# Pooled products of a hybrid decoder step: one fp32 product per chunk, or three float32r products of split operands

## The chip, the core and the metric

One core of a Trainium2 chip runs the whole kernel. The metric is the device time of one execution in microseconds (us). The engines are TensorE (PE, its weight loads PEld), VectorE (DVE), ScalarE (ACT), GpSimd (POOL) and SyncE (SP). SP, ACT and POOL issue the transfers, each in the order of its own queue.

## What is computed

One inference step of a decoder layer: 1024 prompt tokens and 8 sample tokens, model width 1024, all in fp32. An RMS norm and one projection feed two halves. One is sparse attention in three branches, with paged caches for the sample tokens. The other is a pooling mixer in four channel groups of 128, and it is what changes here:

```python
def pool_mixer(u_ext, n_out, w_pool, pool_scale):
    ...
    mean = (csum[:, le - n_out + 1:] - lo) / (end[:, None] - start).astype(f32)
    d = (mean - uf[:, le - n_out:]).reshape(n, n_out, N_POOL_GROUPS, POOL_GROUP_DIM)
    y = jnp.einsum('nlgc,gcd->nlgd', d, w_pool).reshape(n, n_out, D_POOL)
    return y * pool_scale

def combine(x, o_attn, za, o_pool, zp, w_out):
    a = o_attn * jax.nn.silu(za.astype(jnp.float32))
    b = o_pool * jax.nn.silu(zp.astype(jnp.float32))
    mix = jnp.concatenate([a, b], axis=-1).astype(x.dtype)
    return x + jnp.einsum('nlm,md->nld', mix, w_out)
```

The trailing windows of the four groups are 2, 4, 8 and 16 tokens; the sample tokens take their history from `state_pool`.

## The kernel before

**Exact products from rounded operands.** Nearly every product takes its operands as float32r. `split_w` (L142) makes a high part by a copy on ScalarE and a low part by a subtraction on VectorE, and three matmuls, high x high, high x low and low x high, add up in PSUM. The pooled product (L849) is the exception before the change: plain fp32 operands and one call of matmul per chunk.

**The stages.** Up to about 180 us the kernel normalizes and transposes the input, projects keys and values, compresses the cache and projects the queries. From about 180 to 285 us it runs the pooling groups (L801 to L859) and, between them, `decode` (L548), the attention of the sample tokens. From 285 us on come the prompt's attention units with the output projection as filler.

**A pooling group g.** `load_tile` (L387) loads and splits 128 columns of weights for u. `feat_unit` (L400) projects them in three token chunks of 384, 384 and 264 (CHUNKS), each 24 matmuls (L404 to L406) into one of two PSUM accumulators that `ps_any` (L71) takes in turns. ScalarE copies each into u (L808). Three transposes (L810 to L812) serve the new pool state; the third turns the state rows, spt, for the window sums of the sample tokens (us, L815 to L817). VectorE adds u to itself shifted, one to four times (L824), and makes dd, mean minus u (L832). Then zp is projected in the same three chunks (L842), and `silu2` (L409) forms the gate sz: a tanh on ScalarE (L411), a multiplication on VectorE (L412). The three pooled products (L849) follow, and bb is product x scale x gate: on VectorE for two chunks (L852), on ScalarE and GpSimd for the third (L856, L857). GpSimd stores bb to b_d in DRAM (L859). The output projection reads it back much later (`split_m`, L1022).

**Tiles.** Before, spt (L707) and pw (L709) are whole and are loaded once by SP; sz and bb hold all 1032 tokens, with one buffer each. The accumulators of the pooled products are three PSUM tiles, "tp".

**Decode.** For each pair of samples GpSimd fetches cache rows into kvx (an indirect gather, L640, or a plain transfer, L644), TensorE transposes the keys (L646), ScalarE copies the values (L651) and GpSimd subtracts (L652). kvx has four buffers.

**The order.** In these stages each engine's order is made by a planner: it simulates the program in time (`TCKW`, L15) and takes ready instructions by priority. Decode and the attention units have high priority (L716, L1176). At run time every engine works in the order so made. Pools are stacked, and a tile that lies where an older one lay waits for that one (`reuse_waits="tile"`).

Of the kernel before, what the change touches and what calls it, by code (L numbers as in the profile page):

```python
# [7 lines left out]
F32 = mybir.dt.float32  # L8
# [33 lines left out]
def hybrid_step_kernel(ctx, tc, xp, xs, ccmp, cslc, cwin, spool, ptab, norm_g, w_in, cmp_pe, cmp_w1,  # L42
# [17 lines left out]
    def ps_t(name="tp"):  # L60
        return psum.tile([128, 512], F32, name=name, tag="tp", bufs=3)
# [80 lines left out]
    def split_w(hi, lo, raw, eng=None):  # L142
        nc.scalar.activation(hi, raw, AF.Copy)
        (eng or nc.vector).tensor_sub(lo, raw, r32(hi))
# [255 lines left out]
    def feat_unit(hi, lo, c):  # L400
        t0, n = CHUNKS[c]
        p = ps_any()
        for k in range(8):
            nc.tensor.matmul(p[:, :n], hi[:, k, :], xh[c][:, k, :], start=k == 0, stop=False)  # L404
            nc.tensor.matmul(p[:, :n], hi[:, k, :], xl[c][:, k, :], start=False, stop=False)  # L405
            nc.tensor.matmul(p[:, :n], lo[:, k, :], xh[c][:, k, :], start=False, stop=k == 7)  # L406
        return p, t0, n
# [295 lines left out]
    pes = ExitStack()  # L703
    pu = pes.enter_context(tc.tile_pool(name="pu", bufs=1, side="right", reuse_waits="tile"))
    pp = pes.enter_context(tc.tile_pool(name="pp", bufs=1, side="right", reuse_waits="tile"))
    bb = pp.tile([128, TOK], F32, name="bb")
    spt = pp.tile([120, 512], F32, name="spt")  # L707
    nc.sync.dma_start(spt, spool.rearrange("b s c -> (b s) c"))
    pw = pp.tile([128, 4, 128], F32, name="pw")  # L709
    nc.sync.dma_start(pw, pool_w.rearrange("g c d -> c g d"))  # L710
    cnt = pp.tile([128, 16], F32, name="cnt")
    nc.gpsimd.iota(cnt, pattern=[[1, 16]], base=1, channel_multiplier=0, allow_small_or_imprecise_dtypes=True)
    nc.vector.reciprocal(cnt, cnt)
# [87 lines left out]
    for g in range(4):  # L801
        w = 2 << g
        hi, lo = load_tile(w_cols(C_U + g * 128))
        u = pu.tile([128, H0 + TOK], F32, name="u", bufs=2)
        nc.vector.memset(u[:, :H0], 0.0)
        for c in range(3):
            p, t0, n = feat_unit(hi, lo, c)
            nc.scalar.activation(u[:, H0 + t0:H0 + t0 + n], p[:, :n], AF.Copy)  # L808
        p = ps_t("ut")
        nc.tensor.transpose(p[:15, :128], u[:, H0 + T - 15:H0 + T], ident)  # L810
        nc.tensor.transpose(p[:NB, 128:256], u[:, H0 + T:H0 + TOK], ident)
        nc.tensor.transpose(p[:, 256:376], spt[:, g * 128:(g + 1) * 128], ident[:120, :120])  # L812
        nc.vector.tensor_copy(utok[:15, g * 128:(g + 1) * 128], p[:15, :128])
        nc.vector.tensor_copy(utoks[:, g * 128:(g + 1) * 128], p[:NB, 128:256])
        us = pp.tile([128, NB, 16], F32, name="us", bufs=2)  # L815
        nc.vector.tensor_copy(us[:, :, :15], p[:, 256:376].rearrange("p (b s) -> p b s", b=NB))
        nc.vector.tensor_copy(us[:, :, 15], u[:, H0 + T:H0 + TOK])  # L817
        cur = u
        step = 1
        k = 0  # L820
        while step < w:
            nx = pp.tile([128, H0 + TOK], F32, name=f"ws{k % 2}")
            nc.vector.memset(nx[:, :H0], 0.0)
            nc.vector.tensor_add(nx[:, H0:H0 + T], cur[:, H0:H0 + T], cur[:, H0 - step:H0 + T - step])  # L824
            cur = nx
            step *= 2
            k += 1
        nc.vector.tensor_reduce(cur[:, H0 + T:H0 + TOK], us[:, :, 16 - w:], axis=AX.X, op=OP.add)
        nc.vector.scalar_tensor_tensor(cur[:, H0:H0 + w - 1], cur[:, H0:H0 + w - 1], float(w),
                                       cnt[:, :w - 1], op0=OP.mult, op1=OP.mult)  # L830
        dd = cur[:, H0:]
        nc.vector.scalar_tensor_tensor(dd, dd, 1.0 / w, u[:, H0:], op0=OP.mult, op1=OP.subtract)  # L832
        if g == 2:
            load_q(0, 0)
            load_q(0, 1)
        if g == 3:
            for _ in stage1(*UNITS[0]):
                pass
        hi, lo = load_tile(w_cols(C_ZP + g * 128))
        sz = pu.tile([128, TOK], F32, name="sz")  # L840
        for c in range(3):
            p, t0, n = feat_unit(hi, lo, c)  # L842
            silu2(sz[:, t0:t0 + n], p[:, :n])
        if g:
            bb = pp.tile([128, TOK], F32, name="bb")
        for c in range(3):
            t0, n = CHUNKS[c]
            p = ps_t("yp")
            nc.tensor.matmul(p[:, :n], pw[:, g, :], dd[:, t0:t0 + n], start=True, stop=True)  # L849
            cs = slice(t0, t0 + n)  # L850
            if c < 2:
                nc.vector.scalar_tensor_tensor(bb[:, cs], p[:, :n], psc[:, g:g + 1], sz[:, cs],  # L852
                                               op0=OP.mult, op1=OP.mult)
            else:

                nc.scalar.activation(bb[:, cs], p[:, :n], AF.Copy, scale=psc[:, g:g + 1])  # L856
                nc.gpsimd.tensor_mul(bb[:, cs], bb[:, cs], sz[:, cs])  # L857
                nc.gpsimd.tensor_copy(bs_t[:, g, :], bb[:, T:])
        nc.gpsimd.dma_start(b_d[g], bb)  # L859
    tc.keep_in_program_order(nc.sync.dma_start(npool_p, utok[:15]))  # L860
    tc.keep_in_program_order(nc.sync.dma_start(npool_s[:, 14], utoks))
    pes.close()
# [419 lines left out]
```

## Time and profile before

| | |
|---|---|
| median of 3 runs | 639.88 us (638.89 to 640.13) |
| profiled execution | 638.69 us |
| its span | 637.0 us |
| TensorE busy in the span | 622.3 us, 98% |
| VectorE, ScalarE, GpSimd busy | 423.4, 367.3, 270.7 us |

The span runs from the first to the last instruction that the profiler shows; the 1.69 us between it and the execution's own time lie around it. Busy time counts an instruction from its start to its modelled end. On TensorE these overlap, so what a matmul costs in a stream is read from the distance between starts. In the waits, "who waited for whom" names the releaser that came last.

### The profile page before, as it was taken

To read this page: it belongs to the slowest core of one execution; us is meant where nothing else is said; L and a number is where in the kernel's file an instruction comes from. 1 tells how busy PE (TensorE), PEld (TensorE's weight loads), DVE (VectorE), ACT (ScalarE), POOL (GpSimd) and SP (SyncE) were. 2 spreads that over 40 slices of the span, in tenths; PEclk is the share of its full clock that TensorE was granted. 3 is DMA by queue.
4 is the path that set the end of the run, shared out by engine and by line. 5 is a ranking of instruction groups with operands and counts; after the bars stand their busy time and mean duration, and the time that the engine had idled before them with its cause. 6 is when DMAs were issued, how large, how long until landed. Compare 5 with 4: busy or idle time off the path is not lost.

```text
span 637.0 us, 12211 instructions
## 1 busy us (share of the span) xinstructions
PE 622.3 (98%) x4160; PEld 578.5 (91%) x4160; DVE 423.4 (66%) x1253; ACT 367.3 (58%) x947; POOL 270.7 (43%) x412
## 2 busy tenths in 40 slices
PE   8999999999999999999999999999999999999995
PEld 5999999999999899999899899789999988898895
DVE  6754234637364647466887999778978787877653
ACT  5654233526223333217887988777877777776652
POOL 6144004314035615005556767645554556444510
PEclk9999999999999999999999999999999999999999
DMA  8436106956224433333313357313113030101101
GB/s 281 152 90 157 34 1 201 314 196 181 74 79 133 138 102 95 92 110 101 100 35 99 100 182 214 107 30 101 37 50 100 18 100 16 67 19 67 51 2 66
DMA packets 63742, 65.13 MB, mean 102 GB/s; under 512 B 4488, under 2 KB 55120, under 8 KB 63640
## 3 DMA queue, kind: packets, MB, share of 16 engines
q1 hardware_dynamic: 53631, 44.55, 23.4%
q0 software_dynamic: 4000, 12.76, 6.2%
q10 hardware_dynamic: 6048, 7.05, 3.2%
q8 instruction: 33, 0.54, 0.4%
q14 instruction: 30, 0.24, 0.1%
HBM read 50.98 MB, written 15.68 MB: 105 GB/s over the span
## 4 chain that ended last, share of the span: by engine, by line
PE 93%; DVE 2%; ACT 1%; issue 1%; DMA 1%; POOL 1%; DVEq 0%; POOLq 0%; ACTq 0%
PE pj L1053 14%; PE S L777 10%; PE tp L902 9%; PE pa L404 7%; PE pa L406 7%; PE pa L405 7%; PE O L920 5%; PE O L919 5%; PE pa L277 4%; PE pa L275 3%; PE pa L276 3%; PE pj L979 2%; PE pj L980 2%; PE pj L981 2%; PE xtp_ps L230 1%; PE pj L1057 1%
## 5 line engine op out<-in xcount | busy, mean ns | idle before, releaser
L908 DVE TENSOR_TENSOR pl<-tp,ph 128x512 fp32r<-128x512 f32 (+1 forms) x136 | 89.9, 670 | 22.7 <-ACT ph L907 22.0
L777 PE MATMUL S<-KT,qt 128*128 128x320 f32 (+10 forms) x400 | 98.2, 346 | 3.0 <-DVE sm L736 3.0
L907 ACT ACTIVATE ph<-tp 128x512 fp32r<-128x512 f32 (+1 forms) x136 | 78.0, 580 | 38.3 <-PE tp L902 28.7
L404 PE MATMUL pa<-x,ws_hi 128*128 128x384 f32 (+1 forms) x288 | 93.7, 325 | 0.0
L406 PE MATMUL pa<-x,ws_lo 128*128 128x384 f32 (+1 forms) x288 | 92.9, 323 | 0.0
L405 PE MATMUL pa<-x,ws_hi 128*128 128x384 f32 (+1 forms) x288 | 92.7, 322 | 0.0
L1053 PE MATMUL pj<-wo,mh 128*128 128x512 f32 (+1 forms) x272 | 84.1, 387 | 0.0
L920 PE MATMUL O<-pl,V 128*128 128x256 f32 x264 | 75.7, 305 | 0.2
L919 PE MATMUL O<-ph,V 128*128 128x256 f32 x264 | 74.0, 296 | 0.0
L777 PEld LDWEIGHTS S<-KT,qt 128*128 128x128 f32 x400 | 63.7, 189 | 9.0 <-DVE sm L736 3.0
L796 POOL TENSOR_SCALAR Ps<-Ps,sm,gates 128x64 f32<-128x64 f32 (+5 forms) x88 | 62.9, 722 | 19.9 <-DVE sm L792 7.3
L789 ACT ACTIVATE Ps<-Ps,sm 128x64 f32<-128x64 f32 (+4 forms) x96 | 60.2, 628 | 16.4 <-DVE sm L736 14.8
L404 PEld LDWEIGHTS pa<-x,ws_hi 128*128 128x128 f32 x288 | 54.2, 188 | 0.5
L405 PEld LDWEIGHTS pa<-x,ws_hi 128*128 128x128 f32 x288 | 54.2, 188 | 0.4 <-issue 0.3
L406 PEld LDWEIGHTS pa<-x,ws_lo 128*128 128x128 f32 x288 | 54.2, 188 | 0.2
L277 PE MATMUL pa<-w_hi,x 128*128 128x256 f32 (+1 forms) x184 | 52.9, 288 | 1.2 <-DVE x L236 1.2
L275 PE MATMUL pa<-w_hi,x 128*128 128x256 f32 (+1 forms) x184 | 53.6, 292 | 0.0
L1053 PEld LDWEIGHTS pj<-wo,mh 128*128 128x128 f32 x272 | 47.2, 188 | 6.1 <-ACT mh L1205 0.3
L920 PEld LDWEIGHTS O<-pl,V 128*128 128x128 f32 x264 | 49.8, 189 | 3.1 <-DVE pl L908 0.6
L276 PE MATMUL pa<-w_lo,x 128*128 128x256 f32 (+1 forms) x184 | 52.4, 285 | 0.0
L1053 PE MATMUL pj<-wo,ml 128*128 128x512 f32 (+1 forms) x136 | 52.1, 383 | 0.0
L919 PEld LDWEIGHTS O<-ph,V 128*128 128x128 f32 x264 | 49.9, 189 | 1.8
(302 smaller groups left out, 1556.1 us busy)
## 6 DMA issues: line engine op xcount, KB each, us to landing
ws_raw<-in_w_in SPq DMA_DIRECT2D x32, 256.0 KB, 3.1
qt<-q_d SPq DMA_DIRECT2D x64, 128.0 KB, 2.9
x_t<-in_x_prompt SPq DMA_DIRECT2D x8, 512.0 KB
wo_raw<-in_w_out SPq DMA_DIRECT2D x8, 512.0 KB, 4.3
r<-in_x_prompt SPq DMA_DIRECT2D x8, 512.0 KB, 3.1
out<-r SPq DMA_DIRECT2D x7, 512.0 KB, 3.1
q_d<-qhl ACTq DMA_DIRECT2D x8, 384.0 KB, 4.0
out<-kvf ACTq DMA_DIRECT2D x5, 512.0 KB, 3.1
```

The source lines that it names most:

```text
L275: nc.tensor.matmul(p[:n, :cn], xh[c][:, k, ts_], hi[:, k, :cn], start=k == 0, stop=False)
L276: nc.tensor.matmul(p[:n, :cn], xh[c][:, k, ts_], lo[:, k, :cn], start=False, stop=False)
L277: nc.tensor.matmul(p[:n, :cn], xl[c][:, k, ts_], hi[:, k, :cn], start=False, stop=k == 7)
L404: nc.tensor.matmul(p[:, :n], hi[:, k, :], xh[c][:, k, :], start=k == 0, stop=False)
L405: nc.tensor.matmul(p[:, :n], hi[:, k, :], xl[c][:, k, :], start=False, stop=False)
L406: nc.tensor.matmul(p[:, :n], lo[:, k, :], xh[c][:, k, :], start=False, stop=k == 7)
L777: nc.tensor.matmul(S[:, :ln], qt[:, f, h, :], KT[:, kv, k0 + a:k0 + a + ln], start=f == 0, stop=f == 1)
L907: nc.scalar.activation(ph[:, :m], tp[:, :m], AF.Copy)
L908: nc.vector.tensor_sub(pl[:, :m], tp[:, :m], r32(ph[:, :m]))
L919: nc.tensor.matmul(O[:, :256], vv, ph[:, a * 256:(a + 1) * 256], start=False, stop=False)
L920: nc.tensor.matmul(O[:, :256], vv, pl[:, a * 256:(a + 1) * 256], start=False, stop=last)
L1053: nc.tensor.matmul(p, a[:, k % 4, :], w, start=first and kk == 0, stop=last and kk == 2)
```

## The change

The weights of the pooled product are loaded by group on GpSimd's queue (pwr) and split once per group (pw, now float32r with two parts). dd is split chunk by chunk into dx, and three float32r matmuls replace the fp32 one. The gate sz, the result bb and the store to b_d go by chunk, and chunk c's product now stands between zp's chunk c and chunk c + 1 in the program. The state rows spt are loaded by group, also by GpSimd. Buffers: spt 2, pwr 1, pw 1, sz 2, dx 1, bb 2.

```diff
-    bb = pp.tile([128, TOK], F32, name="bb")
-    spt = pp.tile([120, 512], F32, name="spt")
-    nc.sync.dma_start(spt, spool.rearrange("b s c -> (b s) c"))
-    pw = pp.tile([128, 4, 128], F32, name="pw")
-    nc.sync.dma_start(pw, pool_w.rearrange("g c d -> c g d"))
...
+        spt = pp.tile([120, 128], F32, name="spt", bufs=2)
+        nc.gpsimd.dma_start(spt, spool.rearrange("b s c -> (b s) c")[:, g * 128:(g + 1) * 128])
...
-        nc.tensor.transpose(p[:, 256:376], spt[:, g * 128:(g + 1) * 128], ident[:120, :120])
+        nc.tensor.transpose(p[:, 256:376], spt, ident[:120, :120])
...
+        pwr = pp.tile([128, 128], F32, name="pwr")
+        nc.gpsimd.dma_start(pwr, pool_w[g])
+        pw = pp.tile([128, 2, 128], F32R, name="pw")
+        split_w(pw[:, 0], pw[:, 1], pwr)
...
-        sz = pu.tile([128, TOK], F32, name="sz")
         for c in range(3):
+            sz = pu.tile([128, 384], F32, name="sz", bufs=2)
             p, t0, n = feat_unit(hi, lo, c)
-            silu2(sz[:, t0:t0 + n], p[:, :n])
-        if g:
-            bb = pp.tile([128, TOK], F32, name="bb")
-        for c in range(3):
-            t0, n = CHUNKS[c]
+            silu2(sz[:, :n], p[:, :n])
+            dx = pp.tile([128, 2, 384], F32R, name="dx")
+            split_w(dx[:, 0, :n], dx[:, 1, :n], dd[:, t0:t0 + n])
             p = ps_t("yp")
-            nc.tensor.matmul(p[:, :n], pw[:, g, :], dd[:, t0:t0 + n], start=True, stop=True)
-            cs = slice(t0, t0 + n)
+            for a, (f, d) in enumerate(((0, 0), (0, 1), (1, 0))):
+                nc.tensor.matmul(p[:, :n], pw[:, f], dx[:, d, :n], start=a == 0, stop=a == 2)
+            bb = pp.tile([128, 384], F32, name="bb", bufs=2)
             if c < 2:
-                nc.vector.scalar_tensor_tensor(bb[:, cs], p[:, :n], psc[:, g:g + 1], sz[:, cs],
+                nc.vector.scalar_tensor_tensor(bb[:, :n], p[:, :n], psc[:, g:g + 1], sz[:, :n],
                                                op0=OP.mult, op1=OP.mult)
             else:
 
-                nc.scalar.activation(bb[:, cs], p[:, :n], AF.Copy, scale=psc[:, g:g + 1])
-                nc.gpsimd.tensor_mul(bb[:, cs], bb[:, cs], sz[:, cs])
-                nc.gpsimd.tensor_copy(bs_t[:, g, :], bb[:, T:])
-        nc.gpsimd.dma_start(b_d[g], bb)
+                nc.scalar.activation(bb[:, :n], p[:, :n], AF.Copy, scale=psc[:, g:g + 1])
+                nc.gpsimd.tensor_mul(bb[:, :n], bb[:, :n], sz[:, :n])
+                nc.gpsimd.tensor_copy(bs_t[:, g, :], bb[:, T - t0:n])
+            nc.gpsimd.dma_start(b_d[g][:, t0:t0 + n], bb[:, :n])
```

## Rows read from the trace of the kernel before

**Rows 1.** The page's head: span, busy time of each engine, granted clock by slice.

```profile
span 637.0 us, 12211 instructions
...
PE 622.3 (98%) x4160; PEld 578.5 (91%) x4160; DVE 423.4 (66%) x1253; ACT 367.3 (58%) x947; POOL 270.7 (43%) x412
...
PEclk9999999999999999999999999999999999999999
```

**Rows 2.** TensorE's waits: waiting line, releaser, total us, times, longest.

```profile
PE S L777 <- DVE sm L736: 3.0, 6, 1.0
...
PE dkt L646 <- DMA kvx<-in_cache_slc_kv,idx: 0.8, 2, 0.6
...
PE tp L902 <- DVE pc L898: 0.4, 1, 0.4
```

**Rows 3.** Stretch 180 to 285: length; busy us of PE, PEld, DVE, ACT, POOL; clock; DMA.

```profile
180.00:285.00 105.00, 104.19 (x665) 97.93 (x664) 60.74 (x159) 32.55 (x79) 36.73 (x51) 1.00 0.39 113
```

**Rows 4.** The chain that ended last: start, us, what (three of five product pieces).

```profile
195.27 1.74 PE yp L849 x6
...
281.24 0.65 PE yp L849 x2
...
282.09 1.29 PE yp L849 x4
```

**Rows 5.** The pooled product's instructions: duration in ns, shortest, median, longest.

```profile
L849 PEld LDWEIGHTS yp<-ws,pw x24: 186/189/190, 194.9 to 282.8; 128*128 128x128 f32 x24
L849 PE MATMUL yp<-ws,pw x24: 386/484/590, 195.1 to 283.0; 128*128 128x384 f32 x16, 128*128 128x264 f32 x8
```

**Rows 6.** TensorE in order of time: start, us, what; 384 columns, then 264.

```profile
199.47 0.33 PE L404 MATMUL pa<-x,ws_hi 128*128 128x384 f32 x1
...
200.51 0.33 PE L404 MATMUL pa<-x,ws_hi 128*128 128x384 f32 x1
200.69 0.33 PE L405 MATMUL pa<-x,ws_hi 128*128 128x384 f32 x1
...
219.19 0.28 PE L406 MATMUL pa<-x,ws_lo 128*128 128x264 f32 x1
219.31 0.28 PE L404 MATMUL pa<-x,ws_hi 128*128 128x264 f32 x1
```

**Rows 7.** The two halves of a split, L143 and L144, 180 to 285 us (ns).

```profile
L143 ACT ACTIVATE ws_hi<-ws_raw x14: 613/623/634, 191.5 to 281.7; 128x512 fp32r<-128x512 f32 x14
...
L144 DVE TENSOR_TENSOR ws_lo<-ws_raw,ws_hi x15: 679/686/828, 179.7 to 283.8; 128x512 fp32r<-128x512 f32 x15
```

**Rows 8.** VectorE (dd, L832) and ScalarE in order of time, idle before in brackets.

```profile
191.28 1.23 DVE L832 SCALAR_TENSOR_TENSOR ws<-ws,u 128x1032 f32<-128x1032 f32 x1
...
192.60 0.37 ACT L411 ACTIVATE sz<-pa 128x264 f32<-128x264 f32 x1
...
199.74 0.42 ACT L651 ACTIVATE vx<-kvx 128x256 fp32r<-128x256 f32 x1 [2.22 <-DMA kvx<-in_cache_slc_kv,idx]
200.07 0.48 ACT L808 ACTIVATE u<-pa 128x384 f32<-128x384 f32 x1
...
201.75 0.49 ACT L808 ACTIVATE u<-pa 128x384 f32<-128x384 f32 x1 [0.83 <-PE pa L406]
```

**Rows 9.** By tile (ns): bb, its store and landing (us); pw and its landing.

```profile
L852 DVE SCALAR_TENSOR_TENSOR bb<-yp,psc,sz x8: 604/610/619, 196.0 to 284.8; 128x384 f32<-128x384 f32 x8
...
L859 POOL DMA_DIRECT2D b_d<-bb x4: 570/583/630, 201.1 to 286.1; - x4
...
DMA to landing us min/median/max: 3.0/3.0/3.5
...
L710 SPq DMA_DIRECT2D pw<-in_pool_w x1: 373/373/373, 181.4 to 181.4; - x1
...
DMA to landing us min/median/max: 4.2/4.2/4.2
```

**Rows 10.** GpSimd in order of time: group 1's first gather.

```profile
207.45 1.87 POOL L640 DMA_INDIRECT kvx<-in_cache_slc_kv,idx  x1 [5.76 <-PE dkt L646]
```

## The prediction

> **What bounds the kernel now.** I read the page's head first. TensorE is busy for 622.3 of 637.0 us, and no slice shows a granted clock under nine tenths [rows 1]. The next view is TensorE's own waits: in the whole span it waits 3.0 us for scores to leave PSUM, 0.8 us for gathered cache rows and 0.4 us for one other thing [rows 2], most of the rest of the 14.7 us lying at the start and the tail. In the stage that is changed, 180 to 285 us, it is busy for 104.19 of 105 us, while VectorE has 60.74, ScalarE 32.55 and GpSimd 36.73 [rows 3]. So the time goes down by what TensorE is spared, and up by whatever makes it wait. The other engines count only through such waits.
>
> The four pooled products lie on the chain that ended last. Three groups run in one piece of 1.74 us, and the fourth is cut by a decode transpose into 0.65 and 1.29 us [rows 4]. That is 3 x 1.74 + 1.94 = 7.16 us.
>
> **The products.** Each plain fp32 product goes out as two instructions, 24 in all, of 484 ns median [rows 5]. Durations overlap on TensorE, so I price by distances between starts. In the projection, which has the float32r form that the change takes up, starts lie 0.17 us apart for 384 columns (more exactly 1.04 us over six, 0.174 each) and 0.12 us for 264 [rows 6]. The change issues nine such matmuls per group: 6 x 0.174 + 3 x 0.12 = 1.40 us, or 5.6 us for four groups against 7.16. TensorE is spared **1.56 us**. From below: if each of the 12 chunks stands alone and pays at its seam what the cut fourth group paid (1.94 - 1.74 = 0.20 us), 12 x 0.20 = 2.4 us come back and the term is +0.8 us. From above, no seam at all and the cut in group 3 gone is just the 1.56. I take 1.5, since the projection's matmuls change weights each time too and show no seam [rows 6].
>
> A weight load lasts 189 ns [rows 5], longer than the 0.174 us from start to start, so on this trace loads run beside the matmuls and do not set their pace. The Trainium skill (Perfetto Trace Analysis, section "Identifying the Most-Contended Engine") would have weight-load time, not matmul time, tell how full TensorE is, and the loads go up from 24 to 36. By that rule the sum would be 36 x 0.189 = 6.8 us against 7.16, a gain of 0.4 us and not 1.5; the starts 0.12 us apart speak against it here.
>
> **The splits.** Twelve chunks of dd and four weights each get a ScalarE copy and a VectorE subtraction. The same split on 128x512 takes 623 ns and 686 ns [rows 7]. By columns, that is 0.47 and 0.51 us for 384, 0.32 and 0.35 for 264, and 0.16 and 0.17 for the 128-column weight. Over four groups ScalarE gets 4 x (0.47 + 0.47 + 0.32 + 0.16) = 5.7 us and VectorE 4 x (0.51 + 0.51 + 0.35 + 0.17) = 6.2 us. Both have room (32.55 + 5.7 and 60.74 + 6.2 of 105 us), so I take nothing. The cover is the projection of the next chunk or group on TensorE. Without it, one chunk's split (0.98 us) would show in front of its product, at most 12 x 0.98 = 11.8 us; there is nothing to gain. dx has one buffer, so a chunk's split waits for the product before it; with 4.2 us of projection per chunk (24 x 0.174) that is covered.
>
> **The gate kept by chunk.** sz has two chunk buffers where it was whole. The third chunk's tanh now waits until the first chunk's bb is done. ScalarE works in order, so u's copies and decode's value copies queue behind that tanh, and TensorE's unit after next waits for its accumulator. In group 0 dd is ready at 191.28 + 1.23 = 192.51 us, and the third tanh starts at 192.60 [rows 8], so here the cover is thinnest. The first bb then comes at 192.51 + 0.47 + 0.51 + 0.52 (three matmuls) + 0.61 (L852 [rows 9]) = 194.6 us. The tanh is 2.0 us late, the accumulator free by 195.6 (0.37 for the tanh, no more than L852's 0.61 for the multiplication). TensorE needs it only after the next group's first unit, 24 x 0.174 = 4.2 us from about 192.5, at 196.7. Cover 1.1 us: nothing, and up to 2.0 us if the cover is gone. The products also move ahead, between the projection's chunks, which changes their place but not their sum.
>
> **The transfers.** SP loses two issues, that of pw 373 ns long [rows 9], with ws_raw and qt behind them, and nobody waited for these two. GpSimd gets 16 more: four spt, four pwr, and 12 pieces of b_d instead of four. At 583 ns each [rows 9] that is 9.3 us on an engine with 68 us free: nothing on the chain, if they stand well. The spt pieces release the transposes and, through us, dd. The pwr pieces release the weight splits. Each b_d piece waits for its bb in GpSimd's order, and what is queued behind it are decode's gathers and value subtractions. I keep both ends for that, from 0 to the 3.5 us worked out in the third rival. The bytes are the same; b_d is read back only in the output stage. The pools shrink by some 0.6 KB a partition, and later tiles lie where they were, so the first gate (zt) or P.V tile may wait for another tile than now. The one wait of that kind that TensorE shows is 0.4 us (L902 for pc) [rows 2]; I take 0 and keep +-0.4.
>
> **The sum.** -1.5 us, and all else covered. The profiled execution took 638.69 us (637.0 of span, 1.69 around it), 1.19 us under the median of the runs, 639.88. It would be 637.2, and on the median **638.4 us**, 0.23% less. A measurement tells about 0.2% (1.28 us) from no change, so this sits just beyond that line.
>
> **The rivals.**
>
> *The saving is eaten by seams and by the gate's cover.* The products stand in 12 pieces and not in one per group, or the third tanh of group 0 holds TensorE. For it: the seam in group 3 and the 0.09 us between dd and tanh in group 0. Against: the gap-free projection rows and 1.1 us of cover. Half the seams (1.2 us) or 1.5 us from the tanh give 639.6 to 639.9. Chance 0.22.
>
> *The plan falls better.* The order on the engines comes from a planner that simulates the program (TCKW, L15), so a change here can shift waits elsewhere. If the gather waits (0.8) and a third of the score waits (1.0) go too [rows 2], it is -3.3: 636.6 us. Nothing in the profile speaks for this direction over the other. Chance 0.12.
>
> *Slower: GpSimd's queue holds the gathers.* A gather issued late lands late. ScalarE stands in order at the value copy until it has landed, and behind it is u's copy, which frees TensorE's accumulator. Group 1 shows this already: ScalarE waits 2.22 us for a gather, u's first copy starts at 200.07 and the second at 201.75 [rows 8], so TensorE has about 201.75 - 200.55 = 1.2 us of cover left. TensorE waits directly as well: 0.8 us for gathered rows [rows 2]. It decides if a b_d piece with its wait, or three issues of 0.58, stand ahead of a gather and make it more than 1.2 us late. Late by 1.2 + 1.75 us at two gather pairs, TensorE stands 3.5 us, and the net is +2.0: 641.9 us. For it: group 1's gathers go out at 207.45, as soon as a buffer is free [rows 10], so there is no reserve. Against: the planner knows these waits, and b_d can be put behind the gathers at no cost.
>
> The Trainium skill's DMA: Bandwidth & Descriptors ("Issuing engine by pattern" and "Rules for kernel authors") speaks on the same side: plain loads belong on Sync, and small ones should be merged. The trace supports it only in part, as a GpSimd store of 516 KB lands in 3.0 us and the SP load of pw in 4.2 [rows 9]; what is dear is the place in the queue. Chance 0.21.
>
> **How the numbers follow.** The forecast, -1.5 us with 1.0 to 2.0 around it, has 0.45. Of that, about 0.30 lies beyond -1.28 us and 0.15 short of it. Faster: 0.30 + 0.12 = 0.42. Same: 0.15 + 0.22 = 0.37. Slower: 0.21. The range reaches down near the better plan (636.4) and up near the slower rival (641.7), which leaves out about half of each, 0.06 and 0.10. The likeliest case's own range is 637.9 to 638.9.
>
> **What the new profile would show.** Right: 36 product matmuls, their starts 0.17 and 0.12 us apart, about 5.6 us on the chain; TensorE busy some 1.5 us less with its waits as now; ScalarE and VectorE up by about 6 us each in the stage. Wrong: product chunks with idle time in front (seams, or waits for dx); a projection matmul waiting for tanh or u's copy; more than 0.8 us of TensorE waits for gathered rows, with GpSimd's gathers behind b_d; other waits for scores in the attention than now.

## The result and the profile after

The changed kernel takes **648.14 us** (647.43 to 649.02, 4 runs) against 640.00 (638.89 to 640.24, 4 runs) for the kernel before, beside which it ran: ratio 1.0131, 95% interval 1.0112 to 1.0151. It is 1.3% slower. The forecast was 638.4 with a range up to 641.7; the measured time lies 6.4 us above its upper end.

The page's head, to be held against [rows 1]:

```profile
span 647.0 us, 12326 instructions
...
PE 626.5 (97%) x4172; PEld 582.2 (90%) x4172; DVE 430.8 (67%) x1269; ACT 373.3 (58%) x963; POOL 274.7 (42%) x428
...
PEclk9999999999999999998999999999999999999998
```

TensorE is busy longer, not shorter, and among the slices in which it works one (291 to 307 us) has a lower granted clock. (The last slice, in which TensorE has finished, shows 0.90 and had 0.91 before.) The stretch that [rows 3] show, 180 to 285 us, looks healthy, with TensorE busy for 103.79 of 105 us, so the loss is not where the change stands:

```profile
180.00:285.00 105.00, 103.79 (x671) 99.22 (x670) 67.10 (x167) 37.98 (x93) 40.81 (x64) 1.00 0.37 108
```

ScalarE and VectorE have 5.4 and 6.4 us more, as forecast. The product itself, by line and by tile (ns; the last two lines say what ended idle time of the engines in front of these instructions, us and times):

```profile
L849 PE MATMUL yp<-dx,pw x36: 281/338/444, 195.3 to 284.8; 128*128 128x384 f32 x24, 128*128 128x264 f32 x12
L143 ACT ACTIVATE dx<-ws x12: 409/524/528, 194.2 to 283.5; 128x384 fp32r<-128x384 f32 x8, 128x264 fp32r<-128x264 f32 x4
L144 DVE TENSOR_TENSOR dx<-ws,dx x12: 419/550/810, 195.6 to 284.1; 128x384 fp32r<-128x384 f32 x8, 128x264 fp32r<-128x264 f32 x4
...
  PE yp L849: 6.0, 5
...
  DVE dx L144: 2.0, 4
```

There are 36 matmuls of float32r length. The splits take 0.52 and 0.55 us for 384 columns, where 0.47 and 0.51 were forecast. The copies into dx wait 6.0 us for the product before (one buffer), and 2.0 us of waiting ends with a low part.

Now the end of the stage. By tile (ns, then the start of the first and the last one): a transpose of decode's first part (dpt), decode's last step on TensorE (dOt) and the attention's scores (S). In the kernel before:

```profile
L614 PE MATMUL dpt<-ident,pd x1: 273/273/273, 202.7 to 202.7; 64*128 64x64 f32 x1
L695 PE MATMUL dOt<-ident,od x1: 271/271/271, 281.8 to 281.8; 64*128 64x64 f32 x1
L777 PE MATMUL S<-KT,qt x400: 221/330/482, 287.4 to 595.4; 128*128 128x320 f32 x39, 128*128 128x352 f32 x21, 128*128 128x288 f32 x16, 128*128 128x512 f32 x11
```

In the changed one:

```profile
L614 PE MATMUL dpt<-ident,pd x1: 271/271/271, 213.4 to 213.4; 64*128 64x64 f32 x1
L695 PE MATMUL dOt<-ident,od x1: 273/273/273, 288.4 to 288.4; 64*128 64x64 f32 x1
L772 PE MATMUL S<-KT,qt x400: 221/327/477, 296.3 to 603.3; 128*128 128x320 f32 x38, 128*128 128x352 f32 x22, 128*128 128x288 f32 x16, 128*128 128x416 f32 x11
```

Read the times behind the commas: dpt is 10.7 us late, dOt 6.6, the first scores 8.9, the last scores 7.9. From first to last score the attention takes 307.0 us, before 308.0. The changed kernel enters the attention late and then takes about as long as before, although it has less left to do there: 45 of the 384-column matmuls that project za, the gate of the attention, stand ahead of its first scores, 24 in the kernel before. At 0.174 us each these 21 are 3.7 us of work brought forward, and they bring back 1.0.

How decode becomes late shows first on GpSimd, in order of time. The kernel before:

```profile
186.42 0.95 POOL L555 MEMSET qx<- 128x1024 f32 x1 [1.55 <-DMA kc_d<-Vcs]
...
189.53 0.98 POOL L640 DMA_INDIRECT kvx<-in_cache_slc_kv,idx  x1 [0.16 <-issue]
...
197.75 0.10 POOL L588 MEMSET cmask<- 64x8 f32 x1
```

The changed kernel:

```profile
188.95 0.54 POOL L805 DMA_DIRECT2D spt<-in_state_pool  x1 [2.22 <-PE ut L809]
189.48 0.97 POOL L555 MEMSET qx<- 128x1024 f32 x1
...
192.56 1.02 POOL L640 DMA_INDIRECT kvx<-in_cache_slc_kv,idx  x1
...
198.29 0.59 POOL L859 DMA_DIRECT2D b_d<-bb  x1
...
203.16 0.57 POOL L859 DMA_DIRECT2D b_d<-bb  x1
203.73 0.13 POOL L588 MEMSET cmask<- 64x8 f32 x1
```

A load of spt stands in GpSimd's order ahead of decode's first memset and waits 2.22 us for a transpose ut. The memset and the first gather come 3.1 and 3.0 us late. Two stores of b_d stand between decode's steps, and the mask that decode's first part needs is finished 6.0 us late. The next 3 us come on VectorE, where other work stands between decode's softmax steps: from the addition of the mask (L611) to the last step (L606) it is 6.4 us and was 3.3 (197.88 to 201.14).

```profile
203.89 0.28 DVE L611 TENSOR_TENSOR pd<-dsc,cmask 64x128 f32<-64x128 f32 x1 [0.24 <-POOL cmask L588]
...
210.33 0.32 DVE L606 TENSOR_SCALAR pd<-pd,dst,g 64x128 f32<-64x128 f32 x1
```

At the end of decode, the seam between the two stages, TensorE's order has nothing to fill in. In order of time, with the idle time in front in brackets, and then 2 us stretches (length, busy time of PE, PEld, DVE, ACT and POOL, granted clock, DMA share, GB/s):

```profile
288.36 0.27 PE L695 MATMUL dOt<-ident,od 64*128 64x64 f32 x1 [1.22 <-DVE od L693]
290.04 0.69 PE L979 MATMUL pj<-x,ws_hi 128*128 128x384 f32 x1 [1.41 <-DVE za L965]
```

```profile
288.00:290.00 2.00, 0.27 (x1) 0.14 (x1) 1.52 (x6) 0.00 (x0) 0.00 (x0) 0.70 0.69 181
290.00:292.00 2.00, 1.96 (x6) 1.96 (x7) 0.00 (x0) 0.00 (x0) 0.00 (x0) 0.50 0.75 209
292.00:294.00 2.00, 2.00 (x8) 2.00 (x7) 0.00 (x0) 0.00 (x0) 0.00 (x0) 0.50 0.56 159
294.00:296.00 2.00, 2.00 (x9) 2.00 (x9) 0.00 (x0) 0.00 (x0) 0.00 (x0) 0.60 0.00 0
```

TensorE is nearly idle from 288 to 290, and its granted clock falls to 0.50, the lower of its two levels (1.2 of 2.4 GHz). The projection of za behind it (L979 to L981), filler that belongs to the attention, runs at 6 to 9 matmuls per 2 us instead of 12. Added up over such stretches between 276 and 310 us, TensorE loses 1.0 us of idle time in the kernel before and nothing to the clock (busy time by what the clock lacks of 1.00). In the changed one it loses 4.3 and 2.9. That is 6.2 of the 10.0 us by which the span grew; of the rest, 2.5 us are idle time behind 310 us and 1.3 us more busy time.

### The profile page after: what moved, and what is told of

It is laid out like the page before. It is cut to its first block, busy times and chain, and to the rows that moved or that the text cites. A ratio compares the mean times of both kernels' runs of the same rounds, so it can differ in the third digit from the quotient of the medians.

```text
span 647.0 us, 12326 instructions
## 1 busy us (share of the span) xinstructions
PE 626.5 (97%) x4172; PEld 582.2 (90%) x4172; DVE 430.8 (67%) x1269; ACT 373.3 (58%) x963; POOL 274.7 (42%) x428
## 4 chain that ended last, share of the span: by engine, by line
PE 56%; DVE 5%; issue 3%; DMA 2%; ACT 2%; POOL 1%; POOLq 0%; DVEq 0%; ACTq 0%
PE pj L1053 12%; PE S L772 9%; PE tp L902 7%; PE O L920 4%; PE O L919 4%; PE pa L406 3%; PE pa L405 3%; PE pa L404 3%; PE pj L979 2%; PE pj L980 2%; PE pj L981 2%; DMA kvx<-in_cache_slc_kv,idx 1%; DMA wo_raw<-in_w_out 1%; PE pj L1057 1%; PE yp L849 1%
## 5 line engine op out<-in xcount | busy, mean ns | idle before, releaser
L1053 PE MATMUL pj<-wo,mh 128*128 128x512 f32 (+1 forms) x272 | 85.6, 389 | 1.2 <-ACT mh L1205 0.8
L784 ACT ACTIVATE Ps<-Ps,sm 128x64 f32<-128x64 f32 (+4 forms) x96 | 60.1, 627 | 21.9 <-DVE sm L731 21.5
L277 PE MATMUL pa<-w_hi,x 128*128 128x256 f32 (+1 forms) x184 | 52.9, 288 | 1.2 <-DVE x L236 1.2
```

The lines of the kernel that those rows point to most:

```text
L784: e = nc.scalar.activation(regs[br], regs[br], AF.Exp, scale=-1.0, bias=sm[:, hh, 0, br:br + 1], accum_out=sm[:, hh, 1, br:br + 1])
L1053: nc.tensor.matmul(p, a[:, k % 4, :], w, start=first and kk == 0, stop=last and kk == 2)
```

## The experiments

Eighteen kernels ran, in five groups; those of a group share the runs of the kernel before (medians 638.66 to 638.78). The row of the changed kernel is the result above, taken beside 640.00, so it compares better by its ratio. None leaves out a part of the computation. "Queue" names who issues the new transfers.

| run | product | queue | us (range) | ratio, 95% interval |
|---|---|---|---|---|
| sp_fp32 | fp32 | SP | 641.54 (640.44 to 645.96) | 1.0049 (1.0028 to 1.0070) |
| fp32_by_chunk | fp32 | GpSimd | 649.83 (649.59 to 651.02) | 1.0167 (1.0150 to 1.0184) |
| changed kernel | split | GpSimd | 648.14 (647.43 to 649.02) | 1.0131 (1.0112 to 1.0151) |
| all_on_sp | split | SP | 645.39 (643.62 to 647.50) | 1.0090 (1.0067 to 1.0112) |
| loads_on_sp | split | loads SP, stores GpSimd | 649.16 (648.88 to 649.42) | 1.0156 (1.0139 to 1.0173) |
| stores_on_sp | split | stores SP, loads GpSimd | 647.11 (645.09 to 647.59) | 1.0117 (1.0095 to 1.0140) |

### Whose queue

The new transfers go to SP instead of GpSimd, all of them (all_on_sp) or the loads or the stores alone:

```diff
-        nc.gpsimd.dma_start(spt, ...)
+        nc.sync.dma_start(spt, ...)
...
-        nc.gpsimd.dma_start(pwr, pool_w[g])
+        nc.sync.dma_start(pwr, pool_w[g])
...
-            nc.gpsimd.dma_start(b_d[g][:, t0:t0 + n], bb[:, :n])
+            nc.sync.dma_start(b_d[g][:, t0:t0 + n], bb[:, :n])
```

> The changed kernel, with all transfers that the change put on GpSimd's queue (spt, pwr, the pieces of b_d) on SP's. Theory A (GpSimd's queue makes decode late; the attention then starts late, TensorE idles at that seam and its clock falls): decode's last transpose L695 comes back from 288.4 to 281 to 284 us, no half clock at the seam, 638 to 641 us against 648.1. Rival B (the splits and the products in pieces, by ScalarE's and VectorE's queues and the single dx buffer, make decode and TensorE late): the seam stays, 645 to 649 us. Rival C (the planner's order falls anywhere at each edit): any time between 636 and 650, with no tie to where decode stands.

> The changed kernel, with spt and pwr on SP's queue, the pieces of b_d still on GpSimd's. Theory A, if the loads in front of decode's memsets and gathers do it: 638 to 641 us; if the pieces of b_d do it (waits for bb in GpSimd's order): 645 to 649 us. Rival B: 645 to 649 us.

> The changed kernel, with the pieces of b_d on SP's queue, spt and pwr still on GpSimd's. Theory A, if the pieces of b_d do it: 638 to 641 us; if the loads do it: 645 to 649 us, with decode's first scores (L609) 3 us late as in the changed kernel. Rival B: 645 to 649 us.

fp32_by_chunk keeps the queue and the chunks, and takes the split away:

```diff
-        pw = pp.tile([128, 2, 128], F32R, name="pw")
-        split_w(pw[:, 0], pw[:, 1], pwr)
...
-            dx = pp.tile([128, 2, 384], F32R, name="dx")
-            split_w(dx[:, 0, :n], dx[:, 1, :n], dd[:, t0:t0 + n])
...
-            for a, (f, d) in enumerate(((0, 0), (0, 1), (1, 0))):
-                nc.tensor.matmul(p[:, :n], pw[:, f], dx[:, d, :n], start=a == 0, stop=a == 2)
+            nc.tensor.matmul(p[:, :n], pwr, dd[:, t0:t0 + n], start=True, stop=True)
```

> The changed kernel with the product back in plain fp32 on pwr and dd (no splits, no dx, no pw), chunks and queues kept. Theory A: decode is as late as in the changed kernel and TensorE has 1.5 us more to do, 647 to 651 us. Rival B: without the splits and pieces the time falls to 638 to 642 us.

sp_fp32 has both edits: chunks, fp32 product, transfers on SP.

> The changed kernel with plain fp32 products (no splits, no dx, no pw) and all of the new transfers on SP's queue; chunks kept. It differs from fp32_by_chunk (649.8 us) in the queue alone. Theory A2 (what counts is when decode ends against the end of the pooling groups' own matmuls; GpSimd's queue is one cause that makes it late, the split products another): decode's last transpose L695 at 281 to 284 us, no half clock behind it, 638 to 641 us. Rival B2 (handling the gate, the products and the store by chunk is itself the cost): 645 us or more. Rival C (the planner's order falls anywhere): any time.

**fp32_by_chunk is slower than the change itself.** So with the transfers on GpSimd the split product is not what made the changed kernel slow: it gives 1.7 us back by the medians (649.83 to 648.14) and 0.36% by the ratios, whose intervals just touch. **sp_fp32 against fp32_by_chunk** is one edit, the queue, and it is worth 8.3 us (sp_fp32 is half a microsecond above the range expected of it). The edit takes with it the order that the planner makes: in fp32_by_chunk 24 matmuls of za stand ahead of dOt, in sp_fp32 and in the kernel before none. The place in the queue and this order were not tried apart. Decode and scores move with the edit. By tile in fp32_by_chunk, then GpSimd in order of time and the same tiles in sp_fp32:

```profile
L695 PE MATMUL dOt<-ident,od x1: 272/272/272, 290.4 to 290.4; 64*128 64x64 f32 x1
L772 PE MATMUL S<-KT,qt x400: 221/328/501, 297.9 to 605.5; 128*128 128x320 f32 x38, 128*128 128x352 f32 x22, 128*128 128x288 f32 x16, 128*128 128x416 f32 x11
```

```profile
190.64 0.99 POOL L640 DMA_INDIRECT kvx<-in_cache_slc_kv,idx  x1 [0.16 <-issue]
...
198.74 0.10 POOL L588 MEMSET cmask<- 64x8 f32 x1
```

```profile
L695 PE MATMUL dOt<-ident,od x1: 271/271/271, 282.7 to 282.7; 64*128 64x64 f32 x1
L772 PE MATMUL S<-KT,qt x400: 243/327/477, 288.0 to 596.6; 128*128 128x320 f32 x38, 128*128 128x352 f32 x22, 128*128 128x288 f32 x16, 128*128 128x416 f32 x11
```

The profile of sp_fp32 began 1.1 us later as a whole (the first matmul of L277, in the projections of the first stage, stands at 18.1 us, at 17.0 in the kernel before and in fp32_by_chunk). Less that 1.1, its first gather, mask, dOt and scores lie within 0.5 us of the kernel before. On GpSimd's queue dOt is 8.6 us later than in the kernel before, the first scores 10.5, and the attention lasts 307.6 us, on SP's 308.6.

With the split product the queue is worth less: all_on_sp, 645.39, is 2.7 us under the changed kernel, and either half of the move alone brings 1.0 us (the stores) or nothing (the loads, 649.16). That spoke against the queue as the whole cause. In all_on_sp decode ends at 286.4 us and the scores begin at 289.2, earlier than in the changed kernel, but they last longer. In loads_on_sp they begin as early and last longer still (all_on_sp, then loads_on_sp):

```profile
L772 PE MATMUL S<-KT,qt x400: 222/347/616, 289.2 to 602.3; 128*128 128x320 f32 x38, 128*128 128x352 f32 x22, 128*128 128x288 f32 x15, 128*128 128x512 f32 x12
L772 PE MATMUL S<-KT,qt x400: 245/347/797, 289.1 to 606.1; 128*128 128x320 f32 x39, 128*128 128x352 f32 x22, 128*128 128x288 f32 x16, 128*128 128x512 f32 x11
```

```profile
PE S L772 <- DMA qt<-q_d: 1.8, 2, 1.6
PE yp L849 <- ACT dx L143: 0.5, 1, 0.5
PE yp L849 <- DVE dx L144: 0.4, 1, 0.4
```

That is 313.1 and 317.0 us instead of 308. So in loads_on_sp the first scores come 7.2 us earlier than in the changed kernel, its first gather is nearly as early as before the change (190.4 against 189.5, and 1.0 of that is a later start of its profile), and the time is no better. With the split product, then, an earlier start of the attention does not by itself bring the time back. TensorE's waits in all_on_sp from 276 to 312 us (total, times, longest) show what is new there: the last group's product waits for its split, with no projection left to cover it, and the scores wait for q tiles, which SP issues from 284.5 us on, behind transfers of the pooling stage (from 273.1 in the kernel before). The clock is at half here too: 2.8 us are lost to it between 276 and 310, and 1.7 more between 400 and 440, where TensorE waits 2.2 us for one ph of ScalarE.

### Which group's split

group_store puts GpSimd's transfers back: one whole bb and one store per group on GpSimd, spt (one buffer) and pwr on SP, the split product kept.

```diff
+        bb = pp.tile([128, TOK], F32, name="bb")
         for c in range(3):
...
-            bb = pp.tile([128, 384], F32, name="bb", bufs=2)
...
-            nc.gpsimd.dma_start(b_d[g][:, t0:t0 + n], bb[:, :n])
+        nc.gpsimd.dma_start(b_d[g], bb)
```

split_g012 and split_g3 are loads_on_sp with the split in groups 0 to 2 or in group 3 alone (`if g < 3:` and `if g == 3:` around both splits, the fp32 product otherwise).

> The changed kernel with its split products, but bb whole and one store per group on GpSimd, and spt and pwr on SP's queue: GpSimd's queue is as before the change. Theory A2: the split products alone make decode late, as in all_on_sp (L695 near 286 us, half clock behind it), 643 to 648 us. Rival B2 (stores by chunk): 638 to 641 us.

> loads_on_sp (649.2 us) with the plain fp32 product in group 3 alone; groups 0 to 2 split. Theory A2: decode is late by then, L695 still near 286 us, half clock, 643 to 649 us. Rival D (it is the last group's own chain that shows: one dx buffer, so split, product and split follow each other when TensorE has nothing else): without it 638 to 641 us.

> loads_on_sp with split products in group 3 alone, plain fp32 in groups 0 to 2. Theory A2: decode stands as before the change (L695 at 281 to 284 us), no half clock, 638 to 641 us. Rival D: the last group's chain shows in full, 643 to 648 us with half clock.

With GpSimd's transfers as before (first gather at 189.3, mask at 197.4), group_store still takes 644.06, so the queue is not all that a split variant pays for. split_g012 takes 648.66 (647.05 to 649.63), ratio 1.0140 (1.0117 to 1.0164), and split_g3 648.14 (647.68 to 651.97), 1.0160 (1.0123 to 1.0198), both near their base. In split_g3 decode and the scores are as early as before the change (dOt 281.6, first scores 286.2), and the attention lasts 316.1 us. The base, loads_on_sp (649.16), was a bad choice, since it has the stores on GpSimd. The same was therefore tried on group_store, with gs_fp32 (no split anywhere) and gs_last (split everywhere but in the last chunk of group 3):

> The variant of 644.1 us (one whole bb and one GpSimd store per group, spt and pwr on SP) with the plain fp32 product in all groups: chunks of gate and the transfers by group are what is left of the change. If the split products are what costs on that base: 639 to 641.5 us, no half clock between 276 and 310 us. If the chunked gate and the transfers cost by themselves: 643 to 645 us.

> The same base, split products in groups 0 to 2, plain fp32 product in group 3. Theory G (the splits of the earlier groups make decode late: dOn stands 28 projection matmuls later in TensorE's order than in the kernel before): 643 to 645.5 us, with half clock at the seam. Theory H (the last group's chain of split, product and store stands alone in front of the attention): 638.5 to 641.5 us, without half clock.

> The same base, split product in group 3 alone. Theory G: decode is back at its place in TensorE's order, 639 to 641.5 us. Theory H: 643 to 645.5 us, TensorE waiting for dx in front of the third chunk's product (0.9 us in the 644.1 us variant) and half clock behind it.

> The same base, split products everywhere but in the last chunk of group 3, which has the plain fp32 product and so needs no dx. Theory H in its narrowest form (the one dx buffer makes the last chunk's product wait 0.9 us, and that hole brings the half clock): 640 to 642 us. Theory G: 643 to 645 us.

| run | us (range) | ratio, 95% interval |
|---|---|---|
| group_store | 644.06 (642.95 to 644.87) | 1.0077 (1.0053 to 1.0101) |
| gs_fp32 | 644.22 (642.12 to 647.62) | 1.0099 (1.0068 to 1.0131) |
| gs_g012 | 648.72 (643.22 to 652.10) | 1.0170 (1.0126 to 1.0213) |
| gs_g3 | 654.01 (652.50 to 654.51) | 1.0237 (1.0220 to 1.0254) |
| gs_last | 647.68 (645.93 to 648.46) | 1.0128 (1.0105 to 1.0151) |

Theories G and H both fell. The split in all groups costs the same as none (644.1 and 644.2), and the split in one group alone costs 9.8 us more than none. The parts do not add up; every edit gives another plan of the whole stage, which is the likely reason. Two things can be read all the same. First, the spread: the kernel before repeats within 2.5 us, gs_fp32 and gs_g012 spread over 5.5 and 8.9, and roughly the spans go with the mean granted clock. gs_fp32 had 640.4 us at 0.998, 642.8 at 0.996, 642.2 at 0.992 and 645.9 at 0.987. Second, gs_g3 shows a wait that was nowhere before. ScalarE, VectorE and GpSimd, in order of time:

```profile
290.78 0.46 ACT L861 ACTIVATE bb<-yp,psc 128x264 f32<-128x264 f32 x1
...
298.56 0.60 ACT L912 ACTIVATE ph<-tp 128x512 fp32r<-128x512 f32 x1 [1.55 <-DMA b_d<-bb]
...
298.60 0.69 DVE L913 TENSOR_TENSOR pl<-tp,ph 128x512 fp32r<-128x512 f32 x1 [2.57 <-DMA b_d<-bb]
...
294.69 0.61 POOL L864 DMA_DIRECT2D b_d<-bb  x1
```

Decode is on time (dOt 281.9), but the last chunk's product now stands behind its split and so behind the start of the attention. Its copy into bb runs in ScalarE's order among the exponentials (L784), its store is issued at 294.69 instead of 286.09, and the attention's first ph and pl, which lie where bb lay, wait until it has landed. g3_tail asked for the copy, its multiplication and the store ahead of the attention:

```diff
-        nc.gpsimd.dma_start(b_d[g], bb)
+                with ExitStack() as hp:
+                    if g == 3:
+                        hp.enter_context(tc.high_priority(2000))
...
+                    nc.gpsimd.dma_start(b_d[g], bb)
```

> The variant with the split product in group 3 alone (654.0 us), where ScalarE's copy of the third chunk into bb, its multiplication and the store of b_d on GpSimd have precedence over the attention. If ph and pl waiting for the late store (1.6 and 2.6 us in front of two instructions, and half clock behind it) are what that variant loses: the store goes out near 289 us instead of 294.7, nothing waits for it, and the time falls by 5 us or more, to 645 to 649 us. If not: 652 to 655 us.

It took 654.10 us (652.86 to 657.11). The priority changed no place in the order: the store was issued at 295.27 and ph waited again (2.17 us). So this run says nothing for or against; that the late store is what gs_g3 loses is argued from its waits and not shown.

### Priority for the whole chain

If the chain is late because decode and the attention have priority over it, the chain can have the same:

```diff
+        with ExitStack() as hp:
+            hp.enter_context(tc.high_priority(1000))
-        hi, lo = load_tile(w_cols(C_ZP + g * 128))
+            hi, lo = load_tile(w_cols(C_ZP + g * 128))
...
```

down to the store of b_d, in the changed kernel (hi_after), in all_on_sp (hi_sp), in group_store (hi_gs) and in the kernel before (hi_before).

> The changed kernel with the gate's projection, splits, products and stores of all four groups at the priority that decode and the attention have (1000), nothing else. Theory E (the loss sits at the seam between decode and attention: the last group's product chain is planned behind decode and the attention, the first za unit is used up early, TensorE runs dry near 285 to 296 us and its clock then falls to half): in the planned order the first scores now come right behind the projection with no za matmul ahead of them, so the half clock at the seam (2.9 us lost) and about 3 of the 4.3 us of idle time go; decode stays late because of GpSimd's queue: 641 to 644 us. Rival F (the products cost what they cost wherever the planner puts them: single dx buffer, longer chain): 646 to 650 us, as the changed kernel.

> The same priority on the variant with spt, pwr and the stores of b_d on SP (645.4 us without it). Theory E: no half clock between 276 and 310 us (2.8 us lost without it), 639 to 641 us. Rival F: 644 to 647 us.

> The same priority on the variant with split products, one whole bb and one GpSimd store per group, spt and pwr on SP (644.1 us without it). Theory E: no half clock between 276 and 310 us (3.4 us lost without it), 638 to 640.5 us, which would be level with the kernel before. Rival F: 643 to 645 us.

> The kernel before with the same priority on its gate, product and store: a control for what the priority does by itself. Theory E: the kernel before has nothing to lose at the seam (1.0 us of idle time there), so 638 to 641 us; if it comes out well under 637 us, what the priority gives is not tied to the split products and the other three runs have to be read against this one.

Measured: 657.52 (ratio 1.0309), 657.44 (1.0288), 666.83 (1.0450) and 663.05 (1.0359; 1.0322 to 1.0395). All are far off. The control is what matters: the kernel before loses 24 us by an edit of its planned order alone, without a changed instruction. Between 276 and 310 us its TensorE is busy for 26.37 of 34 us, where the kernel before has 32.94:

```profile
276.00:310.00 34.00, 26.37 (x164) 24.32 (x164) 19.45 (x74) 12.97 (x51) 9.36 (x22) 0.91 0.38 111
```

### What the clock costs

after_busy is the changed kernel with 15 matmuls whose result nobody reads in the two holes at 287 and 289 us. TensorE's order is otherwise the same up to the first scores; behind them the planner placed some 230 of its 4172 matmuls elsewhere.

```diff
+    wp = ps_o("keep")
+    with tc.high_priority(1000):
+        for b, k in zip(marks, (7, 8)):
+            for _ in range(k):
+                a = nc.tensor.matmul(wp[:, :384], KT[:, 0, :128], KT[:, 0, :384], start=True, stop=True)
...
```

(marks are the last dOn and dOt; each of the matmuls is ordered behind its mark.)

> The changed kernel with 15 float32r matmuls of 384 columns on TensorE whose result nobody reads: seven behind the last dOn, eight behind dOt, where it waits 1.2 and 1.4 us. At 0.174 us each they are 1.2 and 1.4 us of work, so by themselves they cost nothing. If the half clock behind the hole (288 to 296 us) comes from the hole: the clock stays full there, the 2.9 us of clock loss between 276 and 310 us go, and the time is 644.5 to 646 us. If the clock falls for another reason: 648 to 650 us.

```profile
288.62 1.49 PE L869 MATMUL keep<-KT 128*128 128x384 f32 x7
290.04 0.27 PE L696 MATMUL dOt<-ident,od 64*128 64x64 f32 x1
290.24 1.69 PE L869 MATMUL keep<-KT 128*128 128x384 f32 x8
...
296.01 0.81 PE L774 MATMUL S<-KT,qt 128*128 128x192 f32 x6
```

```profile
290.00:292.00 2.00, 2.00 (x12) 1.78 (x11) 1.25 (x5) 0.00 (x0) 0.00 (x0) 1.00 0.74 203
292.00:294.00 2.00, 2.00 (x13) 2.00 (x13) 0.00 (x0) 0.00 (x0) 0.00 (x0) 1.00 0.70 199
294.00:296.00 2.00, 2.00 (x13) 2.00 (x12) 0.00 (x0) 0.00 (x0) 0.00 (x0) 1.00 0.44 126
```

The clock did what was expected: it stays at 1.00 through the seam, and in all five runs the mean is 0.996 to 0.998. From dOt to the first scores it takes 6.0 us instead of 8.0. The time did not follow: **648.84 us** (648.47 to 649.67), ratio 1.0158 (1.0142 to 1.0174), no faster than the changed kernel. In its profile decode was 1.6 us later (dOt 290.0), 1.2 us of which is a later start of the whole profile (first matmul of L277 at 18.0 against 16.8 us), so up to 1.2 us may be owed to that; more than that the filling did not bring. So the hole is what lets the clock fall, and filling it does not bring the 8 us back. The changed kernel's own runs fit that: at a mean clock of 0.992 they took 648.74 and 649.02 us, at 0.995 and 0.996 still 647.54 and 647.43. What remains is decode's lateness and what the attention loses behind it.

## Why the prediction was wrong, point by point

**The products: right.** 36 matmuls at float32r length, and a gain of 1.7 us (by the ratios 0.36%, 2.3 us) from fp32_by_chunk to the changed kernel, where 1.5 was taken. By the rule cited from the Trainium skill (Perfetto Trace Analysis, "Identifying the Most-Contended Engine") it would have been 0.4 us; the medians speak against it, the intervals only just. The gain holds with the transfers on GpSimd. On SP's queue the split costs 3.9 us by the medians (641.54 to 645.39; the intervals just overlap), and on group_store's base nothing (644.22 and 644.06).

**The splits, "I take nothing": wrong at the first and the last chunk.** The cover named, 4.2 us of projection per chunk, held for ten chunks. At the first TensorE waits 0.5 us for a low part, and ahead of the last one the projection is used up: the changed kernel waits 0.4 us there and all_on_sp 0.9. On SP's queue the split costs more than these waits (3.9 us); no run took apart where the rest goes.

**The gate by chunk and the transfers by piece.** sp_fp32 has these alone, on SP, and is 2.8 us slower than the kernel before (0.28% to 0.70%). Nothing was taken, with up to 2.0 for the gate. In its profile TensorE loses 0.1 us more than before at the seam, and 1.7 more between 400 and 440. gs_fp32, with the loads on SP but one store per group on GpSimd, is 5.5 us slower than the kernel before (0.68% to 1.31%).

**The transfers, "nothing on the chain, if they stand well": this is the step that failed.** The rival had the mechanism: GpSimd's queue holds decode. It had the wrong place and the wrong price. It looked for gathers late by 1.2 us in front of a ScalarE copy, and priced two such stalls at 3.5 us, a net of +2.0. What happened is that everything decode does on GpSimd became late from its first memset on. Little of it shows up on the way as a wait of TensorE (1.0 us of idle time from 180 to 276 in fp32_by_chunk), since other matmuls stand in front, 24 of za's among them. The lateness comes due at decode's end, where none are left: dOt 8.6 us late and 11.1 us of time in fp32_by_chunk against the kernel before, 8.3 of them by the edit of the queue. With the split product the same edit is worth 2.7 us, and there the larger part of the loss lies behind the seam: in all_on_sp the scores begin 1.8 us later than before the change, of which 1.0 is a later start of its profile, and last 5.1 us longer. The cause of that stays open. "The planner knows these waits, and b_d can be put behind the gathers at no cost", the argument against this rival, was no argument: the planner put spt's load with its wait ahead of decode.

The rule cited beside that rival (the Trainium skill, DMA: Bandwidth & Descriptors, "Issuing engine by pattern": plain loads and stores belong on Sync) came out right for all the transfers together, by 8.3 us with the fp32 product and 2.7 with the split one, and not for the loads alone (649.16 against 648.14). As far as the traces show it, the reason is the place in the queue, and SP is not free of it either: in all_on_sp the q tiles came late.

**The bounds.** No term of the sum priced the seam. [rows 2] show TensorE waiting 0.4 us for one other thing and [rows 3] a full stage. I read that as cover for the stage's other engines, and it is that inside the stage. The next stage begins when decode and the last group are done, and decode's reserve there was small. The decode transpose that cuts the fourth product in two [rows 4] is dOt, the end of decode, right behind the last projection. What it turns, od, is finished on VectorE (the kernel before, then the changed one):

```profile
278.12 0.28 DVE L693 TENSOR_TENSOR od<-od,dOn 64x128 f32<-64x128 f32 x1
```

```profile
288.03 0.28 DVE L693 TENSOR_TENSOR od<-od,dOn 64x128 f32<-64x128 f32 x1
```

Before, od was ready at 278.40 and dOt stood at 281.81, a reserve of 3.4 us. The change makes od 9.9 us late; the reserve covers 3.4 of them, and dOt is 6.6 us late. The row was read as 0.20 us of seam and not as this.

**The forecast of the profile.** One of its signs of a wrong forecast came true, product chunks with idle time in front (0.5 and 0.4 us). GpSimd's stores do stand among decode's steps, but TensorE's waits for gathered rows, which were to grow with them, fell from 0.8 to 0.2 us. The one that mattered, decode's end, was not on the list.

**What stays open.** The chain 638.7, 641.5 (chunks and pieces on SP), 649.8 (the same on GpSimd), 648.1 (split) accounts for the change in three steps. Along another way the same edits have other prices (split on SP +3.9, queue with split +2.7), so they are not properties of the edits alone. Why the attention lasts 313 us in all_on_sp, 317 in loads_on_sp and 322 in gs_g3 is read from waits at the seam and lower clocks, and no run took those away. No variant beat the kernel before.

## What to carry to other kernels

An engine that is busy 99% of a stage hides lateness of the others only until the stage ends: ask of each chain in it when it must be done for the next stage, and how early it is done now. Here decode was 3.4 us early and came 9.9 us later. Being on time is not enough either: variants that entered the attention in time lost as much inside it. Before the price of a new operation is worked out, look at what stands behind its transfers in the issuing engine's order. And where a planner makes the order, measure what a mere change of order does to the old kernel (here up to 24 us) before a difference of that size is put down to an operation.

## What the runs showed of the chip that was not expected

Two stretches of 1.2 and 1.4 us of waiting, with one transpose between, were followed by 6 us of granted clock at 0.50 to 0.60, in which 384 columns went from 0.174 to 0.32 us. Filling the two stretches kept the clock at 1.00. Some variants also repeat less well than the kernel before: within gs_fp32 the mean clock went from 0.998 to 0.987 and the span from 640.4 to 645.9 us, while the kernel before, beside it, stayed within 636.8 to 638.6 at 0.995 to 0.999. The profile of gs_fp32 is that of its fastest run, so what lowered the clock in the others is not shown.
